# Gathers left out at the start of a loop, a gate operand issued a step later, and a stage's first fetches moved up, in a one-core transformer layer with a retrieval feed-forward

## The chip, the cores and the metric

The kernel runs on one core of a Trainium2 chip. The metric is the device time of one execution in microseconds. TensorE is called PE, its weight loads PEld, VectorE DVE, ScalarE ACT, GpSimd POOL and the queue of SyncE SP. Every engine works through its own queue in order.

## The reference: what is computed

One post-norm decoder layer for 256 tokens of width 2048, in float32: eight differential-attention heads and eight stick-breaking heads on one projection, an output projection with a layer norm, a feed-forward that retrieves single-neuron experts, a second layer norm, then a gated per-layer embedding and a third. The change lies in the feed-forward:

```
q = (xt @ wq).reshape(t, PEER_HEADS, PEER_QDIM)
sa = einsum('thc,nc->thn', qa, sub_keys[0]);  sb = einsum('thc,nc->thn', qb, sub_keys[1])
...
top, sel = lax.top_k(cand, PEER_TOPK)          # 16 of the 16384 = 128 x 128 experts, per head
eidx  = take_along_axis(cidx, sel);  gates = softmax(top)
act   = gelu(einsum('thed,td->the', u[eidx], x))
out   = einsum('the,thed->td', gates * act, v[eidx])
```

Each token uses 8 x 16 = 128 experts, and each expert is one row of 2048 numbers in u and one in v. An expert's index is 128 x (first key) + (second key).

## The kernel before, in words

The feed-forward is computed in two ways side by side.

**Token gathers.** For the first 88 tokens the rows of u and v are gathered per token: one indirect DMA on POOL brings 128 rows of 8 KB (1 MB) into one of four `gb` buffers (L1049), and DVE multiplies them and sums up (L1015 for u, L1025 for v). There are 88 such gathers for u and 88 for v. They are one generator, `sparse_work`, stepped by `gathers(n)`: n is added to an account, and each whole unit in it issues one gather and, once four are under way, the DVE product of the oldest. The rates are constants at the head of the file: `GUL` per block of the listed-u loop (first value for 128-column blocks, second for 168-column ones), `GUE` for its last six blocks, `GV` per v block (part 0, part 1; in each pair the first value is for 128 columns).

**Blocks.** The other 168 tokens go through PE in blocks of 128 experts. For the first 56 values of the first key u is used whole (`u_block`, 56 dense blocks). For the other 72 only experts that some token uses are listed: 48 blocks, 30 that concern only the last 128 tokens (128 columns) and then 18 for all 168. Then follow the v blocks: 39 for part 0 (24 of 128 columns, then 15 of 168), 48 for part 1 (30, then 18).

The *listed-u loop* (the loop over `NBLK[1]` = 48 that calls `turn`, around L1480) fetches u rows with an indirect DMA on POOL into one of five `wf` slots (L1412, tile uf), up to `LEAD` = 4 blocks ahead, transposes them on PE in four quarters (L1453, PSUM bank ps_T), copies each quarter to SBUF on ACT (L1456, uT), and multiplies (L1462, ps_u). An ACT Gelu writes the block's weights (L1494, WL). ps_T and ps_u share four PSUM banks.

**Gates.** Beside that loop, from block 4 on, a generator `all_gates` is stepped, once per quarter block. It builds, for three tokens at a time, one-hot matrices on DVE (eq and ohb, L717), scales eq by a gate value's high part on ACT (hi, L1103) and its low part on DVE (lo, L1105), multiplies them on PE (L1114, L1115, up to two groups later) and scales the activations of the dense blocks, A0 and A1, on DVE (L1123). With a `Places` object (`look`) it also turns ohb on PE, copies it on ACT (oht, L1140) and looks up each expert's place. When A0 and A1 are done they are stored to DRAM (s_w) and `stored` is set; then four more steps follow, one a block, and the rest run in the v blocks.

**The v stage.** `fetch` brings v rows (1 MB) into a `wf` slot (tile vf) or one of `NVX` = 4 extra slots (tile vx, part 0 only); nine in turn. `weights` gathers a part 0 block's weights from s_w (tile wc). In the last four blocks of the listed-u loop fetches 0 to 3 are issued. After the loop the memory of A0 and A1 is closed, vx and wc are opened in its place, and the weights and fetches 4 to 8 are issued. `v_blocks` runs 32 matmul records a block into six PSUM banks (L1512). At the end the token sums are added on PE (L1083).

What sets the order: `keep` (keep_in_program_order) marks instructions whose order the scheduler keeps among themselves; other instructions, and POOL's fetches against one another as the trace shows them, are placed by the scheduler's own timeline. `issue_after` puts an edge behind the last row fetch (`behind`).

Of the kernel before, what the change touches and what calls it, by code (L numbers as in the profile page):

```python
# [19 lines left out]
P = 128  # L20
# [26 lines left out]
NBLK = tuple(map(sum, CAPS))  # L47
# [18 lines left out]

GQ = 2.0
GU, GUF, GUT = 0.80, 0.92, 0.50
GUL, GUE = (1.10, 1.50), 2.20
GV = (0.42, 0.80), (0.42, 0.85)  # L70
GSCALE = 2.0 ** 15
GB = 3

# [4 lines left out]
STAG, LEAD, NVX = 3, 4, 4  # L78
FBC = 12
NZERO = 3  # L80
WF = 5
# [90 lines left out]
def build(tc, a, out):  # L172
    nc = tc.nc
# [800 lines left out]
    def gathers(n):  # L974

        nonlocal due
        due += n
        while due >= 1:
            due -= 1
            run(sparse, 1)  # L980
# [112 lines left out]
    def gate_work(oh, aT, bT, runs, look=None):  # L1093

        def one_hot(t0, n, s0, ns):
            ohb = oh.tile([P, GB, P], F16, name="ohb", tag="ohb", bufs=OHB)
            eq, hi, lo = (oh.tile([P, GB, ns], F16, name=nm, tag=nm, bufs=OHB)
                          for nm in ("eq", "hi", "lo"))
            equal(eq[:, :n], io128[:, s0:s0 + ns], aT[:, t0:t0 + n])
            equal(ohb[:, :n], io128, bT[:, t0:t0 + n])  # L1100
            for j in range(n):
                t = slice(t0 + j, t0 + j + 1)
                keep(nc.scalar.mul(hi[:, j, :], eq[:, j, :], ghf[:, t]))  # L1103
            shape = [P, n, ns // 2, 2]
            keep(nc.vector.tensor_tensor(  # L1105
                lo[:, :n].rearrange("p n (k two) -> p n k two", two=2),
                eq[:, :n].rearrange("p n (k two) -> p n k two", two=2),
                gl2[:, t0:t0 + n, None, :].to_broadcast(shape), op=ALU.mult))
            return ohb, hi, lo

        def product(ps, n, ns, ohb, hi, lo):
            for j in range(n):
                o = ps[:, j * ns:(j + 1) * ns]
                nc.tensor.matmul(o, ohb[:, j, :], hi[:, j, :], start=True, stop=False)  # L1114
                nc.tensor.matmul(o, ohb[:, j, :], lo[:, j, :], start=False, stop=True)  # L1115

        def scale(t0, n, ns, dsts, ps):
            g = ps[:, :n * ns].rearrange("p (t a) -> p a t", t=n)
            c0 = 0
            for At, first in dsts:  # L1120
                dst = At[:, :, t0 - first:t0 - first + n]
                c1 = c0 + At.shape[1]
                keep(nc.vector.scalar_tensor_tensor(dst, g[:, c0:c1], 1.0 / GSCALE, dst,  # L1123
                                                    op0=ALU.mult, op1=ALU.mult))
                c0 = c1

        made, multiplied, turned, picked = [], None, [], None
        todo = [(t0, min(GB, t1 - t0), s0, ns, dsts) for first, t1, s0, ns, dsts in runs
                for t0 in range(first, t1, GB)]
        for group in todo + [None] * (OHB + 2 * (look is not None)):  # L1130
            if group is not None:
                made.append((group, one_hot(*group[:4])))
            if multiplied:
                (t0, n, s0, ns, dsts), ps = multiplied
                scale(t0, n, ns, dsts, ps)
                multiplied = None
            if turned and len(turned[-1]) == 3:
                t0, n, ps = turned.pop()
                oht = oh.tile([P, GB * P], F16, name="oht", tag="oht", bufs=4)
                keep(nc.scalar.copy(oht[:, :n * P], ps[:, :n * P]))  # L1140
                turned.append((t0, n, oht, True))
            if picked:
                look.pick(*picked)
                picked = None
            yield
            ready = made and (len(made) > OHB - 2 or group is None)
            if not (ready or turned):
                continue
            ps = pbank(pa, "ps_G")
            if ready:  # L1150
                group, tiles = made.pop(0)
                t0, n, _, ns, _ = group
                product(ps, n, ns, *tiles)
                multiplied = group, ps
            if look is not None:
                if len(turned) > 1 or not ready:
                    t1, n1, oht, _ = turned.pop(0)
                    o = ps[:, GB * SEG1:]
                    look.find(t1, n1, oht, o)
                    picked = t1, n1, o  # L1160
                if ready:
                    pst = pbank(pa, "ps_turn")
                    for j in range(n):
                        nc.tensor.matmul(pst[:, j * P:(j + 1) * P], tiles[0][:, j, :], ident16,
                                         start=True, stop=True)
                    turned.append((t0, n, pst))
            yield
        assert not (made or multiplied or turned or picked)
# [236 lines left out]
    behind = None  # L1405
# [22 lines left out]
    def fetch():  # L1428
        nonlocal taken
        i, b = order.pop(0)  # L1430
        k = taken % (WF + NVX)
        taken += 1
        if k >= WF and not i and b < NBLK[0] - WF:
            vf = vxp.tile([P, D], F32, name="vx", tag="vx", bufs=NVX)
        else:
            vf = slot("vf")
        rows_of(vf, a["v_rows"], idxV[i], b)
        fetched.append([i, b, vf, WL_of(b) if i else None])

    def weights():  # L1440
        for block in fetched:
            i, b, _, w = block
            if w is None:
                c0, n = cols(i, b)
                w = wcp.tile([P, NDT], F32, name="wc", tag="wc", bufs=WF + NVX + 1)
                rows_of(w, a["s_w"].rearrange("p a t -> (p a) t"), idxW[i], b)
                block[3] = w[:, c0:c0 + n]
# [35 lines left out]
    for b in range(NBLK[1]):  # L1483
        ps = pbank(pp, "ps_u")
        c0, n = cols(1, b)
        for c in range(4):
            turn(4 * b + c + 2)
            rows_mm(ps, turned.pop(0), c, c0, n)
            if b >= 4 and (c or n > P) and not stored:
                run(work, 1)  # L1490
        if stored and begun < 4:
            begun += 1
            run(work, 1)
        keep(nc.scalar.activation(WL_of(b), ps[:, :n], AF.Gelu_apprx_tanh))  # L1494
        if b >= NBLK[1] - LEAD:
            fetch()
        gathers(GUL[n > P] if b < NBLK[1] - LEAD - 2 else GUE)
    pools.close("utp")
    assert stored
    pools.close("a1p", "a0p")  # L1500
    vxp = pools.open("vxp", "right", bufs=1)
    wcp = pools.open("wcp", "right", bufs=1)
    with tc.issue_after(behind.ins):
        weights()
        for _ in range(NVX + 1):
            fetch()
            weights()

# [555 lines left out]
```

## Time and profile before

| | us |
|---|---|
| median of 3 runs (1654.5 to 1661.91) | 1656.95 |
| the profiled execution | 1646.54 |
| its span, first to last instruction | 1644.7 |
| PE busy | 1604.3 |
| DVE busy | 1058.7 |
| ACT busy | 731.3 |
| POOL busy | 583.1 |

Indirect DMAs of POOL move 330.83 of 518.53 MB; the mean over the span is 315 GB/s. The stages in the trace: dense u blocks from 532 us, listed-u loop from 812.6 to 1138.8, v blocks from 1143.3 to about 1535, gates and the third layer norm to the end.

How to read it: the page gives the busy time of each engine and, in 40 slices of 41 us, its busy share in tenths (9 is 90% and more). A wait row says who waited for whom, with total, count and longest. A timeline row is start, duration, engine, line, instruction, and in brackets the idle time before it and what ended that. A window row gives each engine's busy time and instruction count, then the granted PE clock (1.00 is full), the busy share of the 16 DMA engines and GB/s. Matmul records overlap, so their durations add up to more than the time that they take.

### The profile page before, as it was taken

The numbers are of one execution on the slowest core, as the hardware profiler recorded it, in microseconds if no ns is written. First come the engines' busy times: TensorE is split into PE (matmuls) and PEld (weight loads), VectorE is DVE, ScalarE is ACT, GpSimd is POOL, SyncE is SP. The second block draws the span as 40 slices with busy tenths as digits, with TensorE's granted clock in tenths as the row PEclk, the third lists the DMA queues.
The fourth block names the chain that finished last, engine by engine and source line by source line (L and its number), as shares of the span: only waits on it lengthen the run. The fifth ranks groups of instructions, "written<-read, shape, count | busy, mean of one in ns | idle before, by whom it ended". The sixth has DMA issues, their size and how long they took to land. (4 is left out here: it accounts for less than half of the span.)

```text
span 1644.7 us, 30592 instructions
## 1 busy us (share of the span) xinstructions
PE 1604.3 (98%) x11666; PEld 1488.5 (91%) x11666; DVE 1058.7 (64%) x2557; ACT 731.3 (44%) x1740; POOL 583.1 (35%) x542
## 2 busy tenths in 40 slices
PE   9999999999999999999979999998899999999998
PEld 7888888888888999999979999998799999999786
DVE  5555588865378899577668778855476533341777
ACT  5587458753201264857646666632142000000543
POOL 0133123200233423322463434455878564440000
PEclk9999999999999999999989999999999999999999
DMA  8644654475799799999999999998999999996671
GB/s 295 203 157 162 230 172 142 154 287 187 282 409 412 285 421 403 410 375 385 371 387 376 343 349 355 360 401 356 408 406 384 366 402 420 421 402 210 214 260 51
DMA packets 90614, 518.53 MB, mean 315 GB/s; under 512 B 12308, under 2 KB 15444, under 8 KB 38322
## 3 DMA queue, kind: packets, MB, share of 16 engines
q0 software_dynamic: 47984, 330.83, 51.0%
q1 hardware_dynamic: 40750, 182.55, 30.4%
q10 hardware_dynamic: 1728, 3.15, 0.5%
q8 instruction: 92, 1.51, 0.4%
q14 instruction: 60, 0.49, 0.1%
HBM read 508.47 MB, written 10.18 MB: 315 GB/s over the span
## 5 line engine op out<-in xcount | busy, mean ns | idle before, releaser
L133 DVE TENSOR_TENSOR wl<-wf,wh 128x1024 fp32r<-128x1024 f32 (+1 forms) x199 | 212.8, 1092 | 126.9 <-ACT wh L132 125.5
L132 ACT CAST wh<-wf 128x1024 fp32r<-128x1024 f32 (+1 forms) x199 | 172.1, 892 | 243.3 <-DMA wf<-ple_gate 129.5
L1025 DVE SCALAR_TENSOR_TENSOR y<-gb,ew,y 128x2048 f32<-128x2048 f32 x78 | 183.2, 2349 | 127.7 <-DMA gb<-v_rows,eig 127.0
L223 PE MATMUL ps_u<-XF,wf 128*128 128x168 f32 x1632 | 251.1, 310 | 0.0
L223 PEld LDWEIGHTS ps_u<-XF,wf 128*128 128x128 f32 x1632 | 234.6, 190 | 2.2 <-DMA s_gl<-gl 0.2
L1462 PE MATMUL ps_u<-XF,uT 128*128 128x128 f32 (+1 forms) x1536 | 223.9, 290 | 0.2 <-ACT uT L1456 0.2
L1015 DVE SCALAR_TENSOR_TENSOR gb<-gb,xq 128x2048 f32<-128x2048 f32 x88 | 200.7, 2285 | 28.0 <-DMA gb<-u_rows,eig 27.9
L1462 PEld LDWEIGHTS ps_u<-XF,uT 128*128 128x128 f32 x1536 | 202.1, 193 | 0.7 <-ACT uT L1456 0.3
L1512 PE MATMUL ps_v<-WL,vf 128*128 128x128 f32 (+1 forms) x1536 | 196.1, 290 | 3.9 <-DMA vf<-v_rows,idxV 3.6
L1512 PEld LDWEIGHTS ps_v<-WL,vf 128*128 128x128 f32 x1536 | 193.7, 194 | 5.5 <-DMA vf<-v_rows,idxV 4.5
L1049 POOL DMA_INDIRECT gb<-u_rows,eig x88 | 99.6, 1132 | 242.6 <-DVE gb L1015 59.7
L211 PE MATMUL ps_qk<-X,wh 128*128 128x512 f32 x512 | 185.2, 401 | 0.0
L1456 ACT COPY uT<-ps_T 128x512 f32<-128x512 f32 x192 | 111.7, 586 | 106.3 <-PE ps_T L1453 106.1
L1103 ACT ACTIVATE hi<-eq,ghf 128x56 f16<-128x56 f16 (+2 forms) x336 | 87.3, 326 | 138.6 <-DVE eq L717 117.8
L213 PE MATMUL ps_qk<-X,wl 128*128 128x256 f32 x512 | 145.7, 285 | 0.0
L1412 POOL DMA_INDIRECT vf<-v_rows,idxV x73 | 93.9, 1286 | 120.6 <-PE ps_v L1512 88.2
L1049 POOL DMA_INDIRECT gb<-v_rows,eig x88 | 117.5, 1336 | 53.8 <-issue 20.7
L1453 PE MATMUL ps_T<-ident,uf 128*128 128x128 f32 x768 | 116.2, 276 | 5.8 <-ACT WL L1494 5.8
L211 PEld LDWEIGHTS ps_qk<-X,wh 128*128 128x128 f32 x512 | 96.4, 188 | 22.0 <-issue 1.0
L1512 PE MATMUL ps_v<-wc,vf 128*128 128x128 f32 (+1 forms) x800 | 107.3, 293 | 8.2 <-DMA vf<-v_rows,idxV 8.2
L223 PE MATMUL ps_q<-XF,wf 128*128 128x256 f32 x512 | 113.5, 379 | 0.0
L1512 PEld LDWEIGHTS ps_v<-wc,vf 128*128 128x128 f32 x800 | 102.6, 194 | 8.4 <-DMA vf<-v_rows,idxV 8.4
(366 smaller groups left out, 2859.3 us busy)
## 6 DMA issues: line engine op xcount, KB each, us to landing
wf<-peer_u SPq DMA_DIRECT2D x51, 1024.0 KB
wf<-w_qk SPq DMA_DIRECT2D x64, 512.0 KB
wf<-w_out SPq DMA_DIRECT2D x32, 512.0 KB
wf<-peer_wq SPq DMA_DIRECT2D x16, 1024.0 KB
wf<-ple_gate SPq DMA_DIRECT2D x16, 1024.0 KB
wf<-w_v SPq DMA_DIRECT2D x16, 512.0 KB
wf<-w_sv SPq DMA_DIRECT2D x15, 512.0 KB
early<-peer_u SPq DMA_DIRECT2D x5, 1024.0 KB
```

What stands on the lines that cost most here:

```text
L132: self.order(nc.scalar.copy(wh, src))
L133: self.order(nc.vector.tensor_tensor(wl, src, wh.bitcast(F32), op=ALU.subtract))
L211: nc.tensor.matmul(ps, wh[:, j * P:(j + 1) * P], xt[:, dt, :], start=dt == 0, stop=False)
L213: nc.tensor.matmul(ps[:, :T], wl[:, j * P:(j + 1) * P], xt[:, dt, :T], start=False, stop=dt == ND - 1)
L223: nc.tensor.matmul(ps[:, :T - t0], wf[:, dt * P:(dt + 1) * P], xt[:, dt, t0:], start=dt == 0, stop=dt == ND - 1)
L1015: keep(nc.vector.scalar_tensor_tensor(g, g, 1.0, xq[i], op0=ALU.mult, op1=ALU.mult, accum_out=eact[i][:, j:j + 1]))
L1025: keep(nc.vector.scalar_tensor_tensor(ys[i], g, ew[i][:, j:j + 1], ys[i], op0=ALU.mult, op1=ALU.add))
L1049: keep(nc.gpsimd.indirect_dma_start(out=g, out_offset=None, in_=a[kind], in_offset=bass.IndirectOffsetOnAxis(ap=eig[i][:, 0, j:j + 1], axi ...
L1453: nc.tensor.transpose(ps[:, j * P:(j + 1) * P], uf[:, (4 * c + j) * P:(4 * c + j + 1) * P], ident)
L1456: keep(nc.scalar.copy(uT, ps))
L1462: nc.tensor.matmul(ps[:, :n], uT[:, j * P:(j + 1) * P], XF[:, d, NSP + c0:NSP + c0 + n], start=d == 0, stop=d == ND - 1)
L1512: return nc.tensor.matmul(o, vf[:, d * P:(d + 1) * P], w, start=False, stop=last and (d % 3 == 2 or d == ND - 1))
```

## The change

Four things. The listed-u loop makes no token gathers in its first three blocks, and the rates of the loop and of part 1's v blocks are other ones. In `gate_work` the instructions that write hi are issued on ACT after the generator's next yield instead of along with eq, ohb and lo; the products that read hi stay where they are. The memory of A0 and A1 is closed, and vx and wc opened, after block 46 of 48 instead of after the loop, and the weights of the three blocks fetched so far are gathered there; after the loop one fetch fewer is issued. Of the nine places in turn, vx takes places 4 to 7 instead of 5 to 8, so fetch 4 gets an extra slot and fetch 8 a wf slot.

```
-GUL, GUE = (1.10, 1.50), 2.20
-GV = (0.42, 0.80), (0.42, 0.85)
+GUL, GUE = (1.24, 1.55), 1.75
+GV = (0.42, 0.80), (0.37, 0.93)
...
         def one_hot(t0, n, s0, ns):
...
-            for j in range(n):
-                t = slice(t0 + j, t0 + j + 1)
-                keep(nc.scalar.mul(hi[:, j, :], eq[:, j, :], ghf[:, t]))
...
-            return ohb, hi, lo
+            return ohb, hi, lo, eq
+
+        def high(t0, n, hi, eq):
+            for j in range(n):
+                keep(nc.scalar.mul(hi[:, j, :], eq[:, j, :], ghf[:, t0 + j:t0 + j + 1]))
...
             yield
+            if group is not None:
+                _, hi, _, eq = made[-1][1]
+                high(*group[:2], hi, eq)
             ready = made and (len(made) > OHB - 2 or group is None)
...
-        if k >= WF and not i and b < NBLK[0] - WF:
+        if LEAD <= k < LEAD + NVX and not i and b < NBLK[0] - WF:
...
-        gathers(GUL[n > P] if b < NBLK[1] - LEAD - 2 else GUE)
+        if b >= 3:
+            gathers(GUL[n > P] if b < NBLK[1] - LEAD - 2 else GUE)
+        if b == NBLK[1] - 2:
+            assert stored
+            pools.close("a1p", "a0p")
+            vxp = pools.open("vxp", "right", bufs=1)
+            wcp = pools.open("wcp", "right", bufs=1)
+            with tc.issue_after(behind.ins):
+                weights()
     pools.close("utp")
-    assert stored
-    pools.close("a1p", "a0p")
-    vxp = pools.open("vxp", "right", bufs=1)
-    wcp = pools.open("wcp", "right", bufs=1)
     with tc.issue_after(behind.ins):
         weights()
-        for _ in range(NVX + 1):
+        for _ in range(NVX):
             fetch()
             weights()
```

More of the change, by code (lines that the diff above doesn't have):

```diff
@@ L1108, in one_hot, with product @@
                 gl2[:, t0:t0 + n, None, :].to_broadcast(shape), op=ALU.mult))
-            return ohb, hi, lo
-        def product(ps, n, ns, ohb, hi, lo):
+            return ohb, hi, lo, eq
+        def high(t0, n, hi, eq):
+            for j in range(n):
+                keep(nc.scalar.mul(hi[:, j, :], eq[:, j, :], ghf[:, t0 + j:t0 + j + 1]))
+        def product(ps, n, ns, ohb, hi, lo, _):
             for j in range(n):
```

## The prediction, made before the result

> **What bounds the kernel now.** I read the page first (busy shares, the 40 slices), then TensorE's waits, then short windows and the timeline around each of its gaps, then the DMA share of the stages that the change touches.
>
> ```profile
> span 1644.7 us, 30592 instructions
> PE 1604.3 (98%) x11666; PEld 1488.5 (91%) x11666; DVE 1058.7 (64%) x2557; ACT 731.3 (44%) x1740; POOL 583.1 (35%) x542
> PE   9999999999999999999979999998899999999998
> DMA  8644654475799799999999999998999999996671
> ```
>
> PE is busy for 98% of the span, so only two things can shorten it: fewer PE instructions (the change removes none) or fewer gaps. Gaps are 1644.7 - 1604.3 = 40.4 us, and the slices below 9, counted from 0, are 20, 27 and 28 (822 to 863 and 1110 to 1192 us, in and behind the listed-u loop) and the last. DMA stands at 9 in all slices from 12 to 35 but one: a second resource close to its end.
>
> ```profile
> PE ps_v L1512 <- DMA vf<-v_rows,idxV: 11.7, 3, 8.2
> PE ps_G L1114 <- DVE lo L1105: 8.7, 1, 8.7
> PE ps_T L1453 <- ACT WL L1494: 5.8, 2, 4.6
> ```
>
> These waits (total, times, longest) are 26.2 us in four places. I call them A (8.7, gate product), B (5.8, transposes behind ACT), C (8.2, the fifth v block) and D (3.4, a later v block).
>
> ```profile
> 847.70 2.29 DVE L1015 SCALAR_TENSOR_TENSOR gb<-gb,xq 128x2048 f32<-128x2048 f32 x1 [2.67 <-DMA gb<-u_rows,eig]
> 850.00 0.24 DVE L717 TENSOR_TENSOR eq<-io,iaT 128x168 f16<-128x168 f16 x1
> 850.27 0.80 ACT L1103 ACTIVATE hi<-eq,ghf 128x56 f16<-128x56 f16 x3 [11.65 <-DVE eq L717]
> ...
> 845.00:850.00 5.00, 0.00 (x0) 0.00 (x0) 2.33 (x6) 0.00 (x0) 0.93 (x1) 0.53 1.01 428
> 850.00:855.00 5.00, 4.16 (x31) 4.06 (x32) 4.22 (x15) 3.78 (x13) 1.04 (x1) 0.50 1.01 423
> 855.00:860.00 5.00, 5.00 (x45) 4.99 (x45) 4.52 (x15) 3.51 (x9) 3.04 (x2) 0.95 1.00 393
> ```
>
> A: VectorE's queue is in order. The first gate comparison (eq) stands behind token-gather products that wait for their rows to land, at a DMA share of 1.01 (window columns: busy of PE, PEld, DVE, ACT, POOL, then clock, DMA share, GB/s). PE and ACT stop until 850. The clock granted afterwards is 0.50 and 0.95, which loses 4.16 x 0.50 + 5.00 x 0.05 = 2.3 us more. A costs 11.0.
>
> ```profile
> 1110.12 2.35 DVE L1025 SCALAR_TENSOR_TENSOR y<-gb,ew,y 128x2048 f32<-128x2048 f32 x1 [4.88 <-DMA gb<-v_rows,eig]
> 1112.60 0.71 ACT L1103 ACTIVATE hi<-eq,ghf 128x18 f16<-128x18 f16 x3 [7.30 <-DVE eq L717]
> 1113.22 0.29 ACT L1494 ACTIVATE WL<-ps_u 128x168 f32<-128x168 f32 x1
> 1122.60 0.71 ACT L1103 ACTIVATE hi<-eq,ghf 128x18 f16<-128x18 f16 x3 [4.16 <-DVE eq L717]
> 1127.05 0.31 ACT L1494 ACTIVATE WL<-ps_u 128x168 f32<-128x168 f32 x1 [0.50 <-PE ps_u L1462]
> 1133.37 0.31 ACT L1494 ACTIVATE WL<-ps_u 128x168 f32<-128x168 f32 x1 [0.50 <-PE ps_u L1462]
> ...
> 1110.00:1115.00 5.00, 1.44 (x6) 1.45 (x7) 2.84 (x4) 2.10 (x7) 0.94 (x1) 0.65 1.00 421
> 1115.00:1120.00 5.00, 5.00 (x27) 4.95 (x27) 2.35 (x1) 0.93 (x2) 0.00 (x0) 0.66 1.01 426
> ```
>
> B: the same chain one engine on. A late gather holds DVE, DVE holds hi on ACT, hi holds the WL activation and the uT copies behind it, and PE lacks a PSUM bank for its transposes. 5.8 idle, and 1.44 x 0.5 + 5.00 x 0.34 = 2.4 at the low clock: 8.2. Undisturbed, such a block takes 1133.37 - 1127.05 = 6.3 us.
>
> ```profile
> 1131.42 1.00 POOL L1412 DMA_INDIRECT vf<-v_rows,idxV  x1 [0.30 <-issue]
> 1138.58 2.13 POOL L1412 DMA_INDIRECT wc<-s_w,idxW  x1 [0.30 <-issue]
> 1143.51 1.00 POOL L1412 DMA_INDIRECT wc<-s_w,idxW  x1 [0.30 <-issue]
> 1144.81 1.00 POOL L1412 DMA_INDIRECT vx<-v_rows,idxV  x1 [0.30 <-issue]
> 1157.78 1.00 POOL L1412 DMA_INDIRECT vf<-v_rows,idxV  x1 [0.30 <-issue]
> ...
> 1143.29 14.54 PE L1512 MATMUL ps_v<-wc,vf 128*128 128x128 f32 x128
> 1166.01 5.52 PE L1512 MATMUL ps_v<-wc,vf 128*128 128x128 f32 x32 [8.18 <-DMA vf<-v_rows,idxV]
> ...
> 1138.00:1150.00 12.00, 12.00 (x84) 9.61 (x83) 4.19 (x2) 0.31 (x1) 9.57 (x8) 1.00 0.62 218
> ```
>
> C: fetches 0 to 3 are issued by 1131.42 and feed the 128 matmuls from 1143.29. Fetch 4, which needs a wf slot, leaves POOL only at 1157.78, behind weight gathers and four vx fetches; its rows come 8.2 us later. Its 32 matmuls take 5.52 against 14.54 / 4 = 3.64: 1.9 more. C costs 10.1. Meanwhile, from 1138 to 1150, small weight gathers fill POOL's queue and DMA falls to 0.62.
>
> ```profile
> 1360.00 5.47 PE L1512 MATMUL ps_v<-WL,vf 128*128 128x128 f32 x32 [3.37 <-DMA vf<-v_rows,idxV]
> 840.00:1480.00 640.00, 613.38 (x5794) 605.81 (x5793) 383.10 (x1040) 213.03 (x619) 341.17 (x267) 0.98 0.97 384
> 1330.00:1450.00 120.00, 116.23 (x985) 115.03 (x985) 44.20 (x27) 4.43 (x8) 58.42 (x47) 0.99 1.01 421
> ```
>
> D: a v block waits for its rows while DMA runs at 1.01. 3.4 + 5.47 - 3.64 = 5.2. Nothing of A to D lies ahead of 812 us, where the edited stages begin.
>
> **The change, part by part.**
>
> *No gathers in blocks 0 to 2, other rates.* The listed-u loop holds 30 x 1.10 + 12 x 1.50 + 6 x 2.20 = 64.2 steps before, 27 x 1.24 + 12 x 1.55 + 6 x 1.75 = 62.6 after. Ahead of the first eq (block 4) stand about one gather step instead of four. Each step carries one DVE product (2.29) and one 1 MB transfer. Three fewer take 6.9 us of DVE work and the waits between them away, and what remains works on rows that were issued before the loop. A goes: 11.0 taken, at least 6 if one late product stays ahead of eq. The clock loss goes with it.
>
> *The price of that* is paid in blocks 3 to 29, 0.14 gathers more each, and is hidden if DVE has room there:
>
> ```profile
> 855.00:1040.00 185.00, 185.00 (x2075) 183.84 (x2075) 147.32 (x548) 120.24 (x333) 76.08 (x64) 1.00 0.94 357
> 1000.00:1060.00 60.00, 60.00 (x641) 59.29 (x640) 52.61 (x190) 38.52 (x108) 24.29 (x19) 1.00 0.94 363
> DMA to landing us min/median/max: 7.3/9.0/10.8
> ...
> 891.85 1.07 POOL L1412 DMA_INDIRECT uf<-u_rows,idxV  x1 [3.88 <-PE ps_T L1453]
> 898.07 0.99 POOL L1412 DMA_INDIRECT uf<-u_rows,idxV  x1 [3.90 <-PE ps_T L1453]
> ```
>
> (The third line is for token gathers between 855 and 1060, the last two are the fetches of two successive blocks.) 185 us hold some 30 blocks of 6.2 us (898.07 - 891.85), so 0.14 x 30 x 2.35 = 10 us of DVE are added: 147 becomes 157 of 185, 85%. In the tighter 60 us, where 1.50 becomes 1.55, 88% becomes 89%. A row is used three gathers after its issue, at 1.24 a block 3 / 1.24 x 6.2 = 15 us, against landings of at most 10.8. Bounds: nothing, or one A-like stop (11); I take nothing.
>
> *High parts a step later.* The hi instructions (3 a group) are issued on ACT after the next yield; they are moved past one uT copy, past the oht copy, and in the last four steps, one a block, past a whole block with its WL. PE's product reads hi two groups later, so it has room. No other queue is crossed. In those four steps hi has 6.3 us more before it stops ACT: of the two stops in B, 7.30 shrinks to 1.0 and 4.16 to nothing. At 1.75 instead of 2.20 gathers a block DVE is also earlier. But the loop is compressed by A, so gathers may land later against PE. B: 6.5 taken of 8.2, 2 as the low end.
>
> *Weights two blocks ahead, vx for fetches 4 to 7.* Three weight gathers go out on POOL after block 46, ahead of fetch 3 and the gathers of block 47, which are queued behind them; one follows after the loop. A weight gather takes 2.13 beside a running DVE product and 1.00 without: 3 x (2.13 + 0.30) = 7.3 us that fetch 3 may be late at worst. Its block starts 3 x 3.64 = 10.9 us after 1143.3, that is 22.8 us after its issue, which covers 7.3 and a landing of 10.8. Fetch 4 no longer waits for a wf slot and goes out right after the fourth weight gather: 1131.4 + 7.3 + 2 x 2.4 = 1143.5 at the latest, 14 us before its issue now, landing by about 1154, before it is needed at 1157.8. The hole of 1138 to 1150 fills: (1.01 - 0.62) x 12 = 4.7 us of the queue won. The s_w stores that must end before these slots open are needed by the weight gathers anyway. Fetch 8 now takes a wf slot; it is needed four blocks (14.5 us) after fetch 4, the cover that fetch 4 now lacks. C: 10 taken, 5 as the low end, should fetch 8 be late instead.
>
> The Trainium skill, "SBUF — State Buffer", section "SBUF: two separate sides", says that a VectorE operation with two SBUF inputs and a GpSimd operation that reads SBUF lock each other out for a whole instruction. It speaks against moving weight gathers to where gather products still run; the 2.13 against 1.00 above agrees. By it the three moved gathers take 7.3 us of POOL, without it 3 x 1.30 = 3.9, and neither reaches the end.
>
> *v-stage rates.* 0.42 to 0.37 in part 1's first 30 blocks removes 1.5 gathers, and 15 blocks at 0.93 instead of 0.85 add 1.2. D shrinks, but stages ahead of it now run faster against the same queue: 2 taken, -4 to 5.2. In all 1.9 steps move towards the end:
>
> ```profile
> 1475.11 2.35 DVE L1025 SCALAR_TENSOR_TENSOR gb<-gb,ew 128x2048 f32<-128x2048 f32 x1 [5.62 <-DMA gb<-v_rows,eig]
> 1480.09 2.35 DVE L1025 SCALAR_TENSOR_TENSOR gb<-gb,ew 128x2048 f32<-128x2048 f32 x1 [2.63 <-DMA gb<-v_rows,eig]
> 1510.93 0.31 PE L1083 MATMUL ps_y<-sel,y 128*128 128x32 f32 x2
> ```
>
> The sums have 1510.9 - 1482.4 = 28 us of room; the last products stand 5 us apart, so two more need some 10. Hidden.
>
> *Sum.* 11.0 + 6.5 + 10 + 2 = 29.5. Now the queue: 640 us at 384 GB/s are 246 MB, and they have to come in some 610 us, 403 GB/s. 421 was held for 120 us, so bytes allow it; by busy share, 640 x (1 - 0.97 / 1.01) = 25 us is all there is to win. I take 25. The profiled execution took 1646.5 (its span and 1.8 around it); 1621.5 after. The median of the timed runs is 10.4 above it, which no row explains and which I carry over: 1656.95 - 25 = 1632.
>
> **The rivals.**
>
> *The queue gives less* (0.16). A and B bring the v stage forward by 17 us, but the rows for it come no sooner, and waits on vf like C and D return. For it: 0.97 over 640 us. Against: 421 held, and the hole before 1150. If 392 GB/s is what it can do, 246 MB need 627: gain 13, time 1644.
>
> *No room at all* (0.05). If 384 is already the most, every gap closed opens another and the time stays 1657. Against: the rows at 421. The Trainium skill, "DMA: Bandwidth & Descriptors", section "Where 436 GB/s comes from", holds that about 358 GB/s from HBM binds; by it no gain is possible. The 421 of this trace disagrees, and the measurement decides.
>
> *POOL's order isn't the written one* (0.12). Fetch 4 is written ahead of the vx fetches and left 13 us behind them, so the order is the scheduler's; a late fetch 8 would bring C back. Gain 25 - 10 = 15: 1642.
>
> *Slower: DVE falls behind in the gate blocks* (0.06). At 85 to 89% it has little left. If the higher rate pushes landings past 15 us (10.8 at most now), each late row stops DVE, then the lo products, then PE, at A's price of 11. Four such stops less 25: 1676. Against: DMA stands at 0.94 in these blocks and PE never waits there.
>
> **How the numbers follow.** The forecast has 0.61 and 1632; within it the low ends (6, 2, 5, -4 give 9) and the full gains (34.5) lie 16 above and 10 below. A measurement of this kernel tells about 0.5% from no change, 8.3 us: faster means below 1648.7. Forecast 0.60, order 0.11, queue 0.11 of its 0.16: 0.82. Within: 0.12, from the queue, the no-room case and small rests. Slower: 0.06. The range 1615 to 1650 goes five below a full gain and above the queue and order cases; it leaves out the no-room and slower cases and some rest below.
>
> **What would show it.** Right: no PE wait on lo near 840 to 850, ACT's waits on eq in the loop below 3 us each, the first vx issued before 1130 on the new clock, no PE wait over 2 us at the fifth v block, granted clock 1.00 throughout 840 to 1200, DMA at 0.99 or more over the two stages. Wrong: waits on vf or uf of 5 us and more anywhere in the v stage (queue), fetch 8 issued behind its need (order), new waits on lo between blocks 5 and 35 (DVE).

## The result, and the profile after

| | median of 8 runs | lowest to highest |
|---|---|---|
| before | 1659.15 us | 1654.5 to 1663.68 |
| after | 1649.04 us | 1644.04 to 1652.43 |

The ratio is 0.9938 (95% interval 0.9919 to 0.9956): 10 us or 0.6% faster. The forecast was 1632. The profiled execution of after took 1646.52, against 1646.54 for the profiled one of before; its span is the same to the tenth of a microsecond, although, as the rows show, the stalls A, B and C are gone. Three lines of the page of after:

```profile
span 1644.7 us, 30589 instructions
PE 1608.9 (98%) x11666; PEld 1489.9 (91%) x11666; DVE 1057.6 (64%) x2557; ACT 732.6 (45%) x1740; POOL 598.5 (36%) x542
...
PE   9999999999999999999999999999899998999998
```

The slices 20, 27 and 28, which were 7, 8 and 8 or 9 before, are full up to 27; the weak ones are now 28 and 33. In short windows around the old places of A and B (same columns as in the prediction):

```profile
845.00:850.00 5.00, 5.00 (x51) 4.98 (x50) 2.07 (x3) 3.16 (x10) 3.83 (x3) 1.00 1.01 424
850.00:855.00 5.00, 5.00 (x58) 4.98 (x58) 4.90 (x20) 3.98 (x10) 3.21 (x2) 1.00 1.01 423
...
1110.00:1115.00 5.00, 5.00 (x40) 5.00 (x39) 2.66 (x3) 3.17 (x9) 4.08 (x4) 1.00 1.01 413
1115.00:1120.00 5.00, 5.00 (x36) 4.80 (x35) 2.06 (x1) 1.23 (x3) 4.09 (x4) 1.00 1.01 407
```

PE is busy throughout at full clock, with the DMA engines at 1.01 as before. And GpSimd's timeline:

```profile
1115.68 2.25 POOL L1416 DMA_INDIRECT vx<-v_rows,idxV  x1 [0.30 <-issue]
...
1126.65 0.99 POOL L1416 DMA_INDIRECT vx<-v_rows,idxV  x1 [0.30 <-issue]
...
1134.40 1.00 POOL L1416 DMA_INDIRECT vf<-v_rows,idxV  x1 [0.30 <-issue]
```

Fetch 4 (the first of these rows) leaves at 1115.68, 42 us earlier than before (1157.78), and fetch 8 (the last row shown) at 1134.40; its rows are used from 1160.75 on. So all that the change was to do happened; of the signs named for it only two fail, the full clock up to 1200 (0.94 from 1080 on, below) and the DMA share of 0.99 (0.96 from 840 to 1480). What TensorE waits for instead (total, times, longest):

```profile
PE ps_v L1520 <- DMA vf<-v_rows,idxV: 6.7, 6, 1.7
PE ps_v L1520 <- issue: 5.8, 12, 1.1
PE ps_G L1115 <- DVE WL L1124: 4.0, 4, 2.5
PE ps_G L1115 <- issue: 2.2, 2, 1.7
```

The second and the fourth row are a kind of idle time that the first profile of before has nowhere: TensorE waits for nothing that the profile shows. Its timeline at the first of these places:

```profile
1133.86 0.70 PE L1520 MATMUL ps_v<-wc,vf 128*128 128x128 f32 x4 [0.28 <-issue]
1135.29 0.47 PE L1520 MATMUL ps_v<-wc,vf 128*128 128x128 f32 x2 [0.73 <-issue]
1136.00 0.27 PE L1520 MATMUL ps_v<-wc,vf 128*128 128x128 f32 x1 [0.24 <-issue]
1136.71 0.71 PE L1520 MATMUL ps_v<-wc,vf 128*128 128x128 f32 x4 [0.44 <-issue]
```

In the middle of a v block, whose first matmuls have run on the same rows and weights, the next group of matmuls starts 0.71 or 1.43 us after the start of the one before (1136.00 - 1135.29, 1135.29 - 1133.86). I call these the steps. They were the riddle of this case.

### The profile page after: what moved, and what is told of

Read it like the earlier page. It is cut to its first block, busy times and chain, and to the rows that moved or that the text cites. A ratio compares the mean times of both kernels' runs of the same rounds, so it can differ in the third digit from the quotient of the medians.

```text
span 1644.7 us, 30589 instructions
## 1 busy us (share of the span) xinstructions
PE 1608.9 (98%) x11666; PEld 1489.9 (91%) x11666; DVE 1057.6 (64%) x2557; ACT 732.6 (45%) x1740; POOL 598.5 (36%) x542
## 4 chain that ended last, share of the span: by engine, by line
PE 81%; DMA 5%; issue 4%; DVE 3%; POOL 3%; another core or an unknown queue 2%; ACT 1%; POOLq 0%; ACTq 0%; SPq 0%; DVEq 0%
PE ps_u L223 15%; PE ps_v L1520 13%; PE ps_u L1466 9%; PE ps_qk L211 7%; PE ps_q L223 7%; PE ps_T L1457 4%; PE ps_qk L213 4%; DMA vf<-v_rows,idxV 3%; PE ps_v L230 2%; PE ps_v L232 2%; PE ps_v L231 2%; PE ps_gate L230 1%; PE ps_gate L232 1%; PE ps_gate L231 1%
## 5 line engine op out<-in xcount | busy, mean ns | idle before, releaser
L1049 POOL DMA_INDIRECT gb<-u_rows,eig x88 | 103.1, 1171 | 237.0 <-DVE gb L1015 58.4
L1416 POOL DMA_INDIRECT vf<-v_rows,idxV x72 | 101.3, 1407 | 105.7 <-PE ps_v L1520 81.5
L1416 POOL DMA_INDIRECT uf<-u_rows,idxV x48 | 68.7, 1432 | 112.7 <-PE ps_T L1457 103.6
```

Of the source, the lines that this page charges most:

```text
L1049: keep(nc.gpsimd.indirect_dma_start(out=g, out_offset=None, in_=a[kind], in_offset=bass.IndirectOffsetOnAxis(ap=eig[i][:, 0, j:j + 1], axi ...
L1416: behind = keep(nc.gpsimd.indirect_dma_start(out=dst, out_offset=None, in_=src, in_offset=bass.IndirectOffsetOnAxis(ap=idx[:, b:b + 1], ax ...
```

## The experiments

Theory 1, formed from the trace of after: the new stalls are made by the order of TensorE's queue. In its v stage stand runs of 30 and 18 gate-product matmuls (five and three groups) without v matmuls between them, at most 12 before; a group waits until VectorE has scaled the one before it (the waits on WL). Theory 2: the steps cost it, they follow the burst of fetches ahead of the v stage, and they are part of nearly every execution. Theory 3, formed after the twelfth run: they belong to some chips, and hide there what the change wins. The rival from the prediction: the DMA queue has no more to give. Ratios are to the kernel before on the same chip, with 95% intervals.

**The three parts.** The rates alone, the high parts alone, weights and slots alone, and the first and third together:

```
e1_rates      GUL, GUE, GV as after; `if b >= 3:` ahead of the loop's gathers
e2_hi         high(...) behind the yield
e3_vx         vx at places LEAD to LEAD + NVX - 1; a1p, a0p closed and weights() after block 46
e4_rates_vx   e1_rates and e3_vx
```

> The kernel before with the gather rates alone changed (no token gathers in the first three listed-u blocks, other steps per block); the high gate parts and the weight gathers stay where they were. The stall of TensorE on VectorE's lo near 842 us (8.7 idle and 2.3 of clock) should go. Theory 1 (clumps: the change wins some 21 us up to the start of the v stage and loses it there again in runs of 3 to 5 adjacent gate products, which wait for VectorE's scale between them): the order of this kernel has no such run of more than two groups, so the gain of the first stall is kept, about 9 to 11 us: 0.994 of before. Rival (the DMA queue has no more to give, and whatever comes earlier waits later for its rows): the gain is lost again to waits on vf in the v stage, 0.999 to 1.001.

> The kernel before with the high gate parts alone a step later; rates and weight gathers as before. The stall on lo near 842 stays, since lo is VectorE's and in the same place; ScalarE's waits on eq at the end of the listed-u loop (7.3 and 4.2 us) shrink. Theory 1 gives at most the 5.8 us that TensorE's transposes waited behind ScalarE, 0.996 to 0.999 of before, as its order has no runs of more than two gate products. The rival (DMA queue) gives 0.999 to 1.001.

> The kernel before with the weight gathers two blocks ahead and the extra slots for fetches 4 to 7 alone. The wait of 8.2 us at the fifth v block should go, and 1.9 of its slow matmuls: up to 10 us. Theory 1: the order of this kernel has two runs of three adjacent gate products in the v stage, worth about 4 us in all, so 5 to 7 us are left: 0.996 of before. The rival (DMA queue): the same rows come late at later blocks, 0.999 to 1.001.

> The whole change without its middle part: rates and weight gathers as changed, the high gate parts as before. Theory 1 (clumps): the order of this kernel has no run of more than two adjacent gate products in the v stage, so what the whole change lost there, 10 us idle and some 4.5 of clock between 1185 and 1240, is kept: a further 8 to 14 us below the whole change, 0.986 to 0.989 of before, less what is left of the stall behind ScalarE (up to 6). Theory 2 (TensorE stutters for nothing that the profile shows, near 1134 to 1147 and 1164 to 1167, whatever the order of the gate products): the stutter stays and the time is within 4 us of the whole change, 0.992 to 0.996. Rival (DMA queue): the same time as the whole change, and the new idle time is on vf.

Measured: e1 0.9905 (0.9879 to 0.993), e2 1.0001 (0.9985 to 1.0018), e3 1.0034 (1.0019 to 1.005), e4 0.9947 (0.9928 to 0.9965). The parts add up: -16, 0 and +6 us make the whole change's -10. The rates alone come out below the whole change (0.9905 against 0.9938, intervals that overlap a little); the last part, forecast at -10, costs 6 or 7 us, alone or on top of the rates. Theory 1 has it wrong in the fourth kernel, which has no long run of gate products and yet the whole change's time. All four profiles have steps (6.6 to 10.2 us of ps_v waits that end in issue). In the second, the hi instructions still stop ScalarE for 7.9 us behind eq, and TensorE's wait on the WL activation is 5.2 us, so the high parts alone do not take B away:

```profile
PE ps_T L1457 <- ACT WL L1498: 5.2, 1, 5.2
```

**The kernel before once more, the halves of the last part, and the change without it.**

```
b_again       no edit
e6_weights    e1_rates, and weights() after block 46; slots as before
e7_slots      e1_rates, and vx at places LEAD to LEAD + NVX - 1
e8_rates_hi   e1_rates and e2_hi
```

> The kernel before once more, unchanged, for a second profile. In the five profiles taken since the first one, TensorE's instructions of the v stage come 0.7 us apart for stretches of 2 to 15 us while the profile shows nothing that they wait for (the rows that end in issue: 5.8 in the whole change, 10.2 with the rates alone, 6.6, 8.2 and 8.1 in the others); the first profile of the kernel before has none. Theory 2: such stretches are part of nearly every execution, and the first profile of before was one without them, which is why its span is 10 us under the median of its runs: this profile shows 5 to 12 us of such idle time in the v stage and a time of 1655 to 1662. Rival: they come with the change, because transfers and TensorE meet there at another time; this profile has none and its other waits add up to 10 us more than the first one's.

> The rates of the change, and of its last part only the weight gathers two blocks ahead; the v slots stay as before, the high parts too. With the rates alone the time was 0.9905 of before, with rates, weights and slots 0.9947. If the weight gathers cost the 7 us (they take places among the eight gathers that may be under way on the queue, ahead of the rows of the first v blocks and of token gathers), this one is at 0.994 to 0.996; if the slots do, at 0.989 to 0.992.

> The rates of the change, and of its last part only the extra v slots for fetches 4 to 7; the weight gathers stay behind the loop. If the slots cost the 7 us (the rows of the v stage are fetched earlier, at the cost of the token rows, which then come later, and part 1's blocks wait for their own rows as in the whole change, 6.7 us), this one is at 0.994 to 0.996; if the weight gathers do, at 0.989 to 0.992.

> The change without its last part: rates and high parts a step later. The stop of TensorE behind ScalarE (4.7 us with the rates alone) should go. If what is gained ahead of the v stage stays, 0.987 to 0.989 of before, a few us under the rates alone; if the v stage takes it back (the queue, or the stretches without a visible wait), the same as the rates alone, 0.990 to 0.992.

Measured, on another chip: b_again 1660.61 in its one run, span 1658.8; e6 0.9913 (0.9893 to 0.9934), e7 0.9912 (0.9896 to 0.9928), e8 0.9888 (0.9868 to 0.9907). TensorE's waits in the second profile of before:

```profile
PE ps_v L1512 <- issue: 9.9, 14, 1.2
PE ps_G L1114 <- DVE lo L1105: 8.9, 1, 8.9
PE ps_T L1453 <- ACT WL L1494: 5.9, 2, 4.6
PE ps_v L1512 <- DMA vf<-v_rows,idxV: 3.4, 1, 3.4
```

A, B and D stand as in the first profile (8.7, 5.8, 3.4). C, the 8.2 us on vf at the fifth v block, is not there: 9.9 us of steps stand in its place. Its timeline shows them in the third and fourth v block, from 1157 on:

```profile
1162.06 1.08 PE L1512 MATMUL ps_v<-wc,vf 128*128 128x128 f32 x3 [1.15 <-issue]
1164.18 0.56 PE L1512 MATMUL ps_v<-wc,vf 128*128 128x128 f32 x1 [1.04 <-issue]
1165.57 0.37 PE L1512 MATMUL ps_v<-wc,vf 128*128 128x128 f32 x1 [0.82 <-issue]
```

While TensorE crawls, the fifth block's rows land. So an execution of before that takes what the timed runs take has no C to remove, and the steps lie between it and the first profile (1646.5). e6 is the exception that fits: its profile has next to no steps (1.1 us), and C is back with 6.3 us on vf. Neither half of the last part costs what both cost (e6 and e7 lie within 2 us of the rates alone), and rates and high parts without it have the lowest ratio so far. The rates alone ran on the chip before, so these comparisons go by ratio.

**Runs of gate products, and the burst.**

```
e14_hi_slots  e8_rates_hi, and vx at places LEAD to LEAD + NVX - 1
e15_hi_weights  e8_rates_hi, and weights() after block 46
e13_nvx2      e8_rates_hi with NVX = 2
e10_spread    e8_rates_hi, and
     with tc.issue_after(behind.ins):
         weights()
-        for _ in range(NVX + 1):
-            fetch()
-            weights()
+        fetch()
+        weights()
...
-            while order and len(fetched) <= (ahead if ... else LEAD):
-                fetch()
-                weights()
+            for _ in range(2):
+                if order and len(fetched) <= (ahead if ... else LEAD):
+                    fetch()
+                    weights()
```

> The whole change without the weight gathers two blocks ahead: rates, high parts a step later, and the v slots for fetches 4 to 7. Rates and high parts alone gave 0.9888 of before, the whole change 0.9938. TensorE's order in this kernel holds the same runs of five and three adjacent gate products in the v stage as the whole change (30, 30, 18 and 18 matmuls against at most 12 without the slots). Theory 1 (these runs, which wait for VectorE's scale between their groups, take back what the first parts won): 0.993 to 0.995, with waits of ps_G on WL and eq of some 6 us and the low clock after them. Rival (the weight gathers ahead cost it, or the two only together): 0.988 to 0.990.

> The whole change without the v slots for fetches 4 to 7: rates, high parts a step later, weight gathers two blocks ahead. No run of more than two adjacent gate products in its order. Theory 1: as rates and high parts alone, 0.988 to 0.990 of before. Rival (the weight gathers ahead cost the 8 us): 0.993 to 0.995.

> Rates and high parts, the slots as before, but the fetches that were written as a burst of five ahead of the first v block are taken at most two a block; on GpSimd's queue four of the v rows then leave ahead of fetches 1 to 3 and of the weight gathers, which go out ten in a row, and the next rows come one at a time between token gathers. Theory 2 (TensorE's unexplained 0.7 us steps follow the end of the burst in which rows and weights of eight blocks leave within some 14 us, and last while the queue works it off): the steps shrink from 9.6 us to under 4 and the time is 0.983 to 0.987 of before. Rival (they have to do with the v stage itself, whatever is fetched): 7 us or more of them, 0.988 to 0.991.

> Rates and high parts with two v slots instead of four beside the five of the weights' tag, so that the burst ahead of the first v block has two fetches less and the fetches run two blocks less ahead in part 0. Its order has runs of 26 and 18 adjacent gate products. Theory 2: the unexplained steps shrink by the 5 us that two fetches of 1 MB take at 420 GB/s. Theory 1: the runs cost some 6 us again in waits of ps_G on WL. Together within 3 us of rates and high parts alone, 0.987 to 0.991; if rows then come late at the v blocks (rival: the lead of the fetches decides), waits on vf of over 8 us and 0.992 to 0.997.

Measured: e14 0.9887 (0.9872 to 0.9901), e15 0.9876 (0.986 to 0.9893), e10 0.9925 (0.9908 to 0.9942), e13 0.9865 (0.9842 to 0.9888). These four ran on a third chip, and there the kernel before took 1648.6 instead of 1660 to 1661, near the first profile's 1646.5. None of the four profiles has a step. Theory 1 falls here: e14 has the whole change's runs of gate products and loses 1.7 us on WL and 1.1 on eq. In e13 the two slots fewer cost nothing: 3.0 us on vf, against the rival's 8, and 1.6 on WL, against theory 1's 6. What e10 says on theory 2 was void here, as there was no step to shrink; its order has a wait of 7.2 us on the WL activation instead.

**The whole change on a chip without steps.** The whole change and the change without its last part, unedited, side by side:

> The whole change once more. On the chips of the first runs the kernel before took 1659 to 1661 and nearly every profile has the unexplained 0.7 us steps of TensorE in the v stage (9.9 us in the second profile of before); on the chip of the last four runs it took 1648.6, like the first profile of before (1646.5), and not one of four profiles has such a step. If this call's chip has no steps: theory 3 (the steps hide what the change wins, as they stand where the fifth v block's wait stood): the whole change is at 1624 to 1630 beside 1648, 0.985 to 0.989. Rival (the last part of the change costs 8 us on every chip): 1634 to 1640, 0.992 to 0.994. If the chip has the steps: 0.993 to 0.995 again.

> Rates and high parts without the last part, once more, to stand beside the whole change on the same chip. Without the steps: theory 3 gives 0.987 to 0.991, with the fifth v block's wait of some 6 to 8 us back, so at or above the whole change; the rival gives 0.985 to 0.989, 8 us below it. With the steps: 0.988 to 0.990 and 8 us below the whole change.

Measured: before 1648.19, whole change 1625.15, ratio 0.9861 (0.9841 to 0.9881); without the last part 1629.62, 0.9884 (0.9862 to 0.9906). The chip has no steps, and here the whole change wins 23.0 us, as theory 3 expects. The change without the last part lies 4.5 us above it; the two intervals overlap, but the profiles show the difference in the expected place. First the waits of the whole change, then those without its last part:

```profile
PE ps_v L1520 <- DMA vf<-v_rows,idxV: 5.9, 5, 2.4
PE ps_x1T L600 <- ACT XF L549: 2.0, 1, 2.0
PE ps_G L1115 <- DVE WL L1124: 1.7, 5, 0.5
```

```profile
PE ps_v L1517 <- DMA vf<-v_rows,idxV: 10.7, 5, 6.5
```

Without the last part C is back: one wait of 6.5 us on vf. With it the first blocks run through; the timeline of the whole change has the last 112 matmuls of the first four blocks, then the four vx blocks, without a gap:

```profile
1128.30 12.75 PE L1520 MATMUL ps_v<-wc,vf 128*128 128x128 f32 x112
1140.89 14.46 PE L1520 MATMUL ps_v<-wc,vx 128*128 128x128 f32 x128
```

**Both kinds of chip once more.** The broken burst, the rates alone, and rates with the last part, unedited:

> Rates and high parts with the burst of fetches ahead of the v stage broken up, once more; on a chip without the 0.7 us steps it took 0.9925 of before. If this chip has the steps (before at 1659 to 1661): theory 2 (they follow the burst of eight fetches) gives under 4 us of waits that end in issue and about 0.988 to 0.990; the rival (they come with the v stage on such a chip, whatever is fetched) 7 us or more and 0.992 or above. If it has none (before at 1647 to 1649): 0.991 to 0.994 and no step, as before.

> The rates alone, once more: 0.9905 of before on a chip with the steps. On a chip without them the first stall (11 us) goes and the waits behind ScalarE and at the fifth v block stay: theory 3 gives 0.991 to 0.994. With the steps 0.989 to 0.992 again.

> Rates and the last part without the high parts, once more: 0.9947 of before on a chip with the steps, 7 us above the rates alone. On a chip without them, theory 3 (the last part takes the fifth v block's wait away, and only the steps hide it) gives 0.986 to 0.990, 4 to 8 us below the rates alone; the rival (the last part costs 7 us on every chip) 0.994 to 0.997. With the steps 0.993 to 0.996 again.

Measured, on a chip with steps (before 1661.75): e10 0.9924 (0.9901 to 0.9947), e1 0.9903 (0.9882 to 0.9925), e4 0.9938 (0.9922 to 0.9954). With steps the last part costs again, 5 us on top of the rates (the two intervals just overlap). What e4 does on a chip without steps was not measured. TensorE's waits in the kernel with the broken burst:

```profile
PE ps_T L1457 <- ACT WL L1498: 7.3, 1, 7.3
PE ps_G L1115 <- DVE WL L1124: 7.3, 3, 4.1
PE ps_v L1516 <- DMA vf<-v_rows,idxV: 2.9, 2, 2.1
PE ps_v L1516 <- issue: 2.5, 6, 0.8
```

The same rates and high parts with the burst, on a chip with steps:

```profile
PE ps_v L1517 <- issue: 7.7, 11, 1.5
```

The steps shrink from 7.7 to 2.5 us with the burst broken up, as theory 2 expects, but the kernel isn't faster: its new order has two stalls, on the WL activation and on VectorE's WL, which stand on the chip without steps too (7.2 and 5.5 us there), and the ratio is the same on both (0.9925 and 0.9924). That the steps follow the burst has this one pair of profiles for it, from two chips, and one profile against it: e6 issues its row and weight gathers in one burst, too, with 1.1 us of steps on ps_v and as much again on the gate products. Theory 2 is not shown.

## Why the prediction was right and wrong

For each stage I summed, over 5 us windows, the window less the product of PE's busy time and granted clock. Stages are cut where TensorE has done the same amount of work. Against the spans the sums are good to about 5 us.

```
                        A: gate    B: loop's  C: first   rest of   D: part 1   tail   sum    span
                        start      end        v blocks   part 0
before, first profile   11.2       8.0        10.0       0.2       5.3         7.2    41.9   1644.7
whole change, no steps  0.0        0.8        0.0        3.1       7.5         7.2    18.6   1623.7
before, with steps      11.3       8.2        18.4       1.0       5.2         7.2    51.3   1658.8
whole change, steps     0.0        0.0        8.2        15.1      6.7         7.4    37.4   1644.7
rates+hi, no steps      0.0        0.3        9.5        0.0       4.2         5.5    19.5   1626.5
rates+hi, steps         1.1        0.0        11.6       4.6       4.1         7.9    29.3   1636.7
```

The wide windows of the four kernels behind the first four lines show it too. Before, first profile:

```profile
1080.00:1200.00 120.00, 106.06 (x880) 102.68 (x879) 58.36 (x102) 31.45 (x91) 80.76 (x59) 0.94 0.97 395
1200.00:1320.00 120.00, 120.00 (x1107) 119.20 (x1106) 73.44 (x219) 30.22 (x116) 82.89 (x64) 1.00 0.98 383
```

The whole change on the chip without steps:

```profile
1080.00:1200.00 120.00, 116.48 (x1043) 113.02 (x1043) 57.05 (x135) 33.81 (x111) 84.00 (x64) 1.00 1.00 405
1200.00:1320.00 120.00, 119.58 (x1079) 118.74 (x1078) 68.62 (x176) 23.54 (x91) 80.57 (x62) 1.00 0.97 380
1320.00:1400.00 80.00, 74.13 (x640) 73.09 (x639) 29.57 (x16) 4.43 (x8) 40.72 (x31) 0.98 1.01 420
```

Before, second profile:

```profile
1080.00:1200.00 120.00, 102.79 (x750) 96.62 (x749) 53.32 (x76) 28.02 (x74) 73.27 (x58) 0.89 0.97 394
1200.00:1320.00 120.00, 118.97 (x1148) 117.91 (x1147) 76.12 (x246) 34.86 (x135) 74.76 (x60) 1.00 0.91 344
```

The whole change, profile of the result:

```profile
1080.00:1200.00 120.00, 108.92 (x873) 104.15 (x873) 43.30 (x79) 24.99 (x74) 80.09 (x64) 0.94 1.00 408
1200.00:1320.00 120.00, 115.92 (x1051) 114.45 (x1051) 70.17 (x228) 32.63 (x126) 63.48 (x51) 0.97 0.81 299
```

In 120 us the first profile of before executes 880 matmuls from 1080 on, the whole change 1043 without steps and 873 with them. From 1200 to 1320 the DMA share falls from 0.97 to 0.81 where the steps and the stalls behind them hold PE back: a v block that isn't finished frees no slot, so the next rows aren't asked for. Between 1180 and 1320 GpSimd waits 21.7 us on v matmuls and 17.2 behind eq with steps, 15.4 and 6.5 without. I read the idle queue there as an effect, which speaks against the rival.

*A, 11.0 forecast.* Right: 11.2 and 11.3 before, 0 after, on both kinds of chip.

*Price of the rates in blocks 3 to 29, nothing forecast.* Right: there is no gap in PE between 860 and 1080 in after.

*B, 6.5 forecast.* Right in size, 7.2 (8.0 to 0.8) without steps and 8.2 with them. But the prediction let the high parts alone do it, and they do not: on the old rates they gave nothing measurable, hi still stopped ScalarE for 7.9 us and the wait on the WL activation stayed at 5.2. The rates alone leave 4.7 and 4.5 us of it in their two profiles. Only together do they take it away, and 0.9905 became 0.9888 (the intervals overlap). In the price of B the first clock term should be 1.44 x 0.35 at the granted 0.65, 0.2 us less.

*C, 10 forecast.* Right for the execution that was read, 10.0 to 0.0. With steps 18.4 becomes 8.2: the late fetch is gone, but not what stood there, and the stage behind it pays.

*Rest of part 0, nothing forecast.* Wrong: 3.1 us without steps, in the runs of gate products, and 15.1 with steps. In the latter profile the waits on WL, issue, eq and hi of the products stand there, with the low clock after them. The first three waits in the longest run of gate products:

```profile
1188.49 0.18 PE L1115 MATMUL ps_G<-hi,ohb 128*128 128x18 f16 x1 [1.70 <-issue]
1189.95 0.18 PE L1115 MATMUL ps_G<-hi,ohb 128*128 128x18 f16 x1 [1.15 <-ACT hi L1110]
1192.78 0.20 PE L1115 MATMUL ps_G<-hi,ohb 128*128 128x18 f16 x1 [2.52 <-DVE WL L1124]
```

The rates and high parts without the last part lose 4.6 there with steps. So on such a chip the last part wins 3.4 in C's stage (11.6 to 8.2) and pays 10.5 in the one behind it, in this pair of profiles. Why is not settled. Without the high parts, rates and last part have no such runs of gate products and a time (0.9947, 0.9938) as high as the whole change's, so the runs alone are not the reason.

*D, 2 forecast.* Wrong in sign: 5.3 becomes 7.5 without steps, within the low end of -4, at a DMA share of 1.01. The experiments show two edits behind it. With steps, before waits 3.4 us on vf between 1315 and 1490, the rates alone wait 0.2 and 0.7 in their two profiles, and with the weights ahead not at all. The slots bring it back (3.3 with the slots alone, 4.3 and 3.8 with the whole last part), and so do the high parts (4.0), with which B goes and the v stage starts earlier. Without steps, rates and high parts have 4.2, with the weights ahead 4.3, and with the slots 6.6 and 5.9. The prediction weighed the rates and a faster stage ahead against D, but not the slots: for them it looked only as far as fetch 8. How the slots delay those rows was not followed.

*Sum, 29.5 cut to 25.* By stages 11.2 + 7.2 + 10.0 - 2.9 - 2.2 = 23.3; the timed gain without steps is 23.0. That the cut to 25 comes this near is in part luck: it was made for the queue, and of what is missing 2.9 stands in the gate products. The queue did give more than before:

```profile
840.00:1455.00 615.00, 605.18 (x5778) 597.14 (x5777) 374.95 (x1028) 216.51 (x620) 367.46 (x264) 1.00 0.99 393
```

The 640 us of before became 615 at 393 GB/s instead of 384. The rule that the prediction weighed, "DMA: Bandwidth & Descriptors", section "Where 436 GB/s comes from", in the Trainium skill, holds that about 358 GB/s from HBM binds; the 393 GB/s over 615 us disagree. They are also more than the 384 that the rival "no room at all" took for the most, so it falls.

*The step that failed.* In the sum it is the term that was left at nothing, the rest of part 0. On chips with steps, like those that timed the kernel, A, B and C give 11.3 + 8.2 + 10.2 = 29.7 by the table, as forecast, but the rest of part 0 takes back 14.1 (1.0 to 15.1) and D 1.5: 14 are left by stages and 10 in the timed runs, and not 25. The sum has no term for a stall behind the fifth block other than D. It could not see one because of its last step: "The median of the timed runs is 10.4 above it, which no row explains and which I carry over". The 10.4 was not a constant that lies beside the kernel. The two profiles of before differ by 14.1 us, and of the 9.4 that the stage sums find of it 8.4 lie in the very stage that the change edits (18.4 against 10.0): steps, absent from the profile that was read, and, by the times and the second profile, present where the kernel was timed. On a chip without steps the forecast 1646.5 - 25 = 1621.5 stands against 1625.5 for the profiled run; on the timed kind the gain is 10 and not 25. What makes the steps, and why the last part costs so much behind them, stays open. Of the rivals, "the queue gives less" named 1644 and came nearest in time, but for a cause that the runs do not show.

Of the two kernels on the table and all the variants, the change without its last part is best where there are steps (0.9888 against 0.9938); without steps the whole change, two v slots (0.9865) and weights ahead without the slots (0.9876) cannot be told apart, and the intervals of the other two (0.9884, 0.9887) overlap with these.

## What to carry to other kernels

When a profiled execution lies outside the range of the timed runs, as 1646.5 against 1654.5 to 1661.9 here, it is not a sample of what is timed: take a second profile, and look for idle time that ends in "issue", before a single stall of it is priced. A stall that is removed only counts if it stands in the executions that are timed; here one of three, C, did not. And read the edits one by one: the parts of this change are worth -16, -3 and +8 us on one kind of chip, and the last turns to about -4 on the other, where the intervals still overlap.

## What the runs showed of the hardware that I had not expected

The same program has, on three or more chips, stretches of up to 14 us in which TensorE's instructions start a multiple of about 0.70 us apart, and on two others none. The two profiles of the kernel before are 14 us of span apart, with the stalls up to the v stage alike within 0.2 us (the first two columns of the table). Nearly all of TensorE's idle time that ends in issue stands between 1133 and 1265 us; between 600 and 1130 no profile has more than 0.6 us of it, and behind 1265 one has 1.0. The steps begin about when a burst of gathers on GpSimd's queue ends: in the profile of the result the last of twelve row and weight gathers in a row leaves at 1130.57, and the first step is at 1133.86; in the second profile of before the burst ends at 1157.51, and the first matmul behind such a wait starts at 1157.09. The chips without steps have such bursts, too. In the second profile of before about a sixth of the records of gather landings is missing (4904 of 6011); in the first, which has no steps, none is. The other profiles divide in the same way: 4876 to 5081 records on chips with steps, 5994 to 6008 on those without. e6 has 4936 with next to no steps, so the loss goes with the chip rather than with the steps. The record doesn't name the chip of the first profile of before; its complete records put it with the chips without steps. Where a landing is not recorded, a wait for it can be shown as issue; the steps in the middle of a v block aren't such waits, those on gate products may be. Late instruction fetches don't fit: both profiles of before have 92 fetch packets of 16 KB, each taking about 1 us, and in the second none falls between 1149 and 1176 us, around the first stretch of steps. Whether the recording makes the steps, or both have one cause, was not tried and stays open; since the timed runs of one kernel differ by chip in the same way as the profiles, they are in the measured times.
